# The second expert table of the sample, layer 0: row sums on VectorE in place of 32-column matmuls

## The chip, the cores and the metric

One Trainium2 chip; the kernel runs on one of its cores. The metric is the device time of one execution in microseconds. A core has a TensorE (PE; its weight loads are listed apart as PEld), a VectorE (DVE), a ScalarE (ACT), a GpSimd (POOL) and a SyncE (SP). SP and POOL here only issue transfers: SP those with fixed addresses, POOL the gathers. Each engine works through its own instruction list in order.

## The reference

Two layers, run over 512 prompt tokens and 128 sample tokens (8 streams of 16). Each layer has a mixer (layer 0: a gated convolution beside windowed attention; layer 1: a gated recurrence) and then a PEER channel mixer, which is what the change touches:

```python
def one_block(xb):                                   # 128 tokens
    q = (xb @ w_query).reshape(TB, 8, 2, 128)
    s = einsum('thpd,hpkd->thpk', q, keys)           # scores against 2 x 128 sub-keys, 8 heads
    sv, si = top_k(s, 16)
    cand = sv[:, :, 0, :, None] + sv[:, :, 1, None, :]
    cand_idx = si[:, :, 0, :, None] * 128 + si[:, :, 1, None, :]
    cv, ci = top_k(cand.reshape(TB, 8, 256), 16)
    idx = take_along_axis(cand_idx.reshape(TB, 8, 256), ci, axis=-1)
    gate = softmax(cv, axis=-1)
    act = gelu(einsum('thkd,td->thk', u_tab[idx], xb))   # first table: 16384 rows of 1024
    return einsum('thk,thkd->td', gate * act, v_tab[idx])    # second table
```

So every token chooses 8 x 16 = 128 experts; each gives a dot product with a row of the first table and adds a weighted row of the second. All is float32.

## The kernel before

The 640 tokens are five groups of 128: the sample ("s"), the prompt's first 128 tokens ("t") and the other 384 ("a", three groups). Groups s and t are computed **sparsely**: POOL gathers one row per token and expert slot. Group a is computed **densely**: all 16384 experts are multiplied with all 384 tokens, 128 experts at a time, and the weights are a matrix that is zero where an expert was not chosen.

The **sparse** part (`sparse_peer`, L823) first turns the ranking of sub-keys into row numbers and gates (`select`, L776, VectorE throughout). Then, for 128 slots, POOL gathers a tile `gu` of 128 rows (one per token, 1024 columns, 0.5 MB) of the first table into one of six buffers (tag "g") and VectorE takes the dot product with the token (L855). The second table follows in one of two ways, by the entry of `SUM` for the group and layer. With a tile name, `weighted` (L877): per slot a gather `gv` by the same row numbers, and one VectorE instruction that multiplies the 128 rows by their tokens' weights and adds to the sum `yv` (L891, the first one without an addition L889); at the end eight transposes and two additions into the activations (L872). With None, which only the sample in layer 0 has, `multiplied` (L903): row numbers and weights are transposed, a gather now fetches the 128 rows of one *token*, and TensorE sums over the partitions with a column of 32 weights of which one is not zero (L933; the column is a window of a zero ring `zr` into which VectorE copies the weights, L926). Four matmuls, for two tokens and two halves of 1024 columns, use four separate 32-column parts of the array and one PSUM bank.

Around that in layer 0 stands this program: `route_p` (L746) ranks the prompt's sub-keys, 16 projections on TensorE and 64 rankings on VectorE (`best`, L738). Then `found` (L970) builds the weight matrix of the three dense groups, 16 **one-hot steps** each, 48 in all. A step takes eight tokens: VectorE makes `ohb` (L988) and six of the `oha` (L1012), ScalarE makes two of them (L1009, L1010), TensorE multiplies them (L1014), ScalarE evacuates into `st` (L1017), and after four steps SP stores two tiles of 1 MB to DRAM (`gd`, L1020). `st` has two buffers. Beside all this run 72 **products ahead** (`ahead`, L956): scores of the last 72 of the 128 expert blocks, each with a load of 0.5 MB (`wraw`), a split into two parts on ScalarE and VectorE (L211, L212 `wlo`), 24 matmuls (L262 to L264), a Gelu (L967) and a store (`sd`, L968). Then the **dense loop** runs over the 128 blocks: its scores are multiplied with `gch`, the weights read back from `gd` (L1050), and then with the second table (L1062).

What stands where is decided twice. The program takes a fixed number of sparse slots per step of other work (`gather`, L1105; `GR` and `GS` are 8 for each projection and each of 12 steps after the routing, `PACE` 3 or 4 per block of the dense loop) and gives them a later priority. From this a scheduler with its own timing of the engines writes each engine's list, and the engines keep to it. The group t begins after the sample is done, with the dense loop; the sample's layer 1 begins at block 56 of it.

Of the kernel before, what the change touches and what calls it, by code (L numbers as in the profile page):

```python
# [8 lines left out]
F32 = mybir.dt.float32  # L9
F32R = mybir.dt.float32r  # L10
I32 = mybir.dt.int32
U32 = mybir.dt.uint32
U16 = mybir.dt.uint16
AF = mybir.ActivationFunctionType
# [4 lines left out]
NEG = -1e30  # L19
LOW = -3e38  # L20
NG = 6
NZ = 3
PACE = ((4,4,4,0)*10+(4,)*90,(3,))
THR = (1, 1, 1)
GM, GR, GS = ((4,),(1,)*40+(2,)*60), (8,8), (8,8)
# [16 lines left out]
LG = 4  # L42
DEEP = (54, 126)
LW = (1000, 1000)
RS = 0
SUM = dict(s=(None, "xn"), t=("vm", "vm"))
KQ = (-1, -1)
FE = ((12, 5, 72), (12, 5, 82))

# [12 lines left out]
def kernel(ctx: ExitStack, tc: tile.TileContext, t: dict):  # L62
    nc = tc.nc
    V, S, P, T, Y = nc.vector, nc.scalar, nc.gpsimd, nc.tensor, nc.sync

    con = ctx.enter_context(tc.tile_pool(name="con", bufs=1))
# [2 lines left out]
    dr = ctx.enter_context(tc.tile_pool(name="dr", bufs=1, space=bass.MemoryType.DRAM))  # L69

    BUFS = {"u4": 2, "uh": 2, "lo": 2, "v4": 4, "vh": 2, "w3": 2, "ge": 2, "g8": 2,
            "nat": 2, "g": NG, "sq": 2, "at": 2, "ai": 5, "vm": 1, "bt": 2, "bi": 2, "el": 2, "els": 2, "ln": 1,
            "gatea": 2, "mr": 1, "xa": 2, "xb": 4}

    def tl(tag, shape, dt=F32, name=None):
        return sb.tile(shape, dt, name=name or tag, tag=tag, bufs=BUFS.get(tag, 1))
# [4 lines left out]
    def bank(tag):  # L81
        return ps.tile([128, 512], F32, name="p" + tag, tag=tag, bufs=1)

    def gps(who):
        turn[who] = turn.get(who, -1) + 1
        return bank(banks[who][turn[who] % len(banks[who])])
# [18 lines left out]
    ident = con.tile([128, 128], F32, name="ident")  # L105
# [50 lines left out]
    V.tensor_tensor(lbt[:, 4], lbt[:, 4], lbt[:, 1], op=OP.subtract)  # L156
    V.tensor_scalar(lbt[:, 5], lbt[:, 4], -1.0, 1.0, op0=OP.mult, op1=OP.add)
    lb, oml = lbt[:, 4], lbt[:, 5]

    zring = []  # L160
    for i in range(NZ):
        z = con.tile([128, 2, 63], F32, name=f"zr{i}")
        V.memset(z, 0.0)
        zring.append(z)


    lay = tl("lay", [128, 1536])
# [652 lines left out]
        k2 = kf.rearrange("p s h k -> p s (h k)")  # L820
        return k2[:, 0], k2[:, 1], gate.rearrange("p h k -> p (h k)")

    def sparse_peer(G, l, xhl, sv, si, quad, acc=None):  # L823


        who = G.name
        xn = tl("xn", [128, 1024], name="xnn")
        for hf in range(2):
            p = gps(who)
            for u in range(4):  # L830
                for v in range(2):
                    T.matmul(p[:, 128 * u:128 * u + 128], xhl(v, 4 * hf + u), identr, start=(v == 0), stop=(v == 1))
            S.activation(xn[:, 512 * hf:512 * hf + 512], p, AF.Copy)
        k1, k2, gate = select(who, sv, si, quad)
        idf = tl("idf", [128, 128])
        V.scalar_tensor_tensor(idf, k1, 128.0, k2, op0=OP.mult, op1=OP.add)
        idt = None
        if acc is None:
            tp = gps(who)[:, :128]
            T.transpose(tp, idf, ident)  # L840
            idt = tl("bt", [128, 128], I32, name="idt")
            V.tensor_copy(idt, tp)
        yield 1
        idx = tl("bi", [128, 128], I32, name="idx")
        after(V.tensor_copy(idx, idf))  # L845
        w = tl("wact", [128, 128])
        rows = []
        for s in range(128 + LG):
            if s < 128:
                rows.append(tl("g", [128, 1024], name="gu"))  # L850
                P.indirect_dma_start(out=rows[s], out_offset=None, in_=t["u"][l],  # L851
                                     in_offset=bass.IndirectOffsetOnAxis(ap=idx[:, s:s + 1], axis=0))
            if s >= LG:
                g = rows[s - LG]
                d = V.tensor_tensor_reduce(out=g, in0=g, in1=xn, scale=1.0, scalar=0.0, op0=OP.mult, op1=OP.add,  # L855
                                           accum_out=w[:, s - LG:s - LG + 1])
                if paced[0] == 2:
                    after(d, 4 - s % 4)
                elif s % 4 == 0 and paced[0]:
                    after(d)  # L860
            yield 1
        S.activation(w, w, AF.Gelu)
        V.tensor_tensor(w, w, gate, op=OP.mult)
        if acc is not None:
            yield from weighted(G, l, idx, w, acc)
        else:
            yield from multiplied(G, l, idt, w)

    def put(G, l, hf, t0, n, q):

        xv = G.x[:, 4 * hf:4 * hf + 4, G.c0 + t0:G.c0 + t0 + n]
        V.tensor_tensor(xv, xv, q, op=OP.add)  # L872
        if l and t0 + n == 128:
            o0 = 512 if G is GS_ else G.c0
            Y.dma_start(t["o_y"][:, 4 * hf:4 * hf + 4, o0:o0 + 128], G.x[:, 4 * hf:4 * hf + 4, G.c0:G.c0 + 128])

    def weighted(G, l, idx, w, acc):  # L877

        y = tl(acc, [128, 1024], name="yv")
        rows = []  # L880
        for s in range(128 + LG):
            if s < 128:
                rows.append(tl("g", [128, 1024], name="gv"))
                P.indirect_dma_start(out=rows[s], out_offset=None, in_=t["v"][l],  # L884
                                     in_offset=bass.IndirectOffsetOnAxis(ap=idx[:, s:s + 1], axis=0))
            if s >= LG:
                e = s - LG
                if e == 0:
                    d = V.tensor_scalar(y, rows[e], w[:, e:e + 1], None, op0=OP.mult)  # L889
                else:  # L890
                    d = V.scalar_tensor_tensor(y, rows[e], w[:, e:e + 1], y, op0=OP.mult, op1=OP.add)  # L891
                if paced[0] == 2:
                    after(d, 4 - s % 4)
                elif s % 4 == 0 and paced[0]:
                    after(d)
            yield 1
        for hf in range(2):
            q = gps("v").rearrange("p (k q) -> p k q", k=4)
            for u in range(4):
                T.transpose(q[:, u], y[:, 512 * hf + 128 * u:512 * hf + 128 * u + 128], ident)  # L900
            put(G, l, hf, 0, 128, q)

    def multiplied(G, l, idt, w):  # L903

        tp = gps("v")[:, :128]
        T.transpose(tp, w, ident)
        wT = tl("wT", [128, 4, 32])
        S.activation(wT.rearrange("p c j -> p (c j)"), tp, AF.Copy)

        tok = [64 * rd + 32 * c + j for rd in range(2) for j in range(32) for c in range(2)]  # L910
        rows = []
        for s in range(128 + LG):
            if s < 128:
                rows.append(tl("g", [128, 1024], name="gv"))
                P.indirect_dma_start(out=rows[s], out_offset=None, in_=t["v"][l],  # L915
                                     in_offset=bass.IndirectOffsetOnAxis(ap=idt[:, tok[s]:tok[s] + 1], axis=0))
            yield 1
            if s < LG:
                continue
            i, c = tok[s - LG], (s - LG) % 2  # L920
            rd, j = i // 64, i % 32
            if c == 0:
                if j == 0:
                    y = gps("v")
                z = zring[j % NZ]
                d = V.tensor_copy(z[:, :, 31:32], wT[:, 2 * rd:2 * rd + 2, j:j + 1])  # L926
                if paced[0] == 2:
                    after(d, 4 - 2 * (j % 2))
                elif j % 2 == 0 and paced[0]:
                    after(d)  # L930
            for hf in range(2):
                q0 = 64 * hf + 32 * c
                T.matmul(y[q0:q0 + 32], z[:, c, 31 - j:63 - j], rows[s - LG][:, 512 * hf:512 * hf + 512], start=(j == 0),  # L933
                         stop=(j == 31), skip_group_check=True, tile_position=(0, q0))
            if j < 31 or c == 0:
                continue
            ys = tl("ln", [128, 512], name="ys")
            S.activation(ys, y, AF.Copy)
            q = gps("v").rearrange("p (k q) -> p k q", k=4)
            for u in range(4):  # L940
                T.transpose(q[:, u], ys[:, 128 * u:128 * u + 128], ident)
            for hf in range(2):
                put(G, l, hf, 64 * rd, 64, q[:, :, 64 * hf:64 * hf + 64])

    def dense_peer(l, xhl, sv, si):

# [147 lines left out]
    mark, paced = [None], [False]  # L1094

    def after(ins, back=0):

        m = marks[-back] if back and len(marks) >= back else mark[0]
        if m is not None:
            tc.add_manual_dep(ins.ins, m.ins.name, mybir.DependencyInfo(  # L1100
                mybir.DependencyClass.NoSync, mybir.DependencyReason.SCHED_ONLY), reason="order")
# [15 lines left out]
    def chain_s(l):  # L1117
# [10 lines left out]
        yield from route_s(l, xhl, sv, si, tags[0])  # L1128
        sp = sparse_peer(GS_, l, xhl, sv, si, tags[2], SUM["s"][l])
        next(sp)  # L1130
# [19 lines left out]
    for l in range(2):  # L1150
# [7 lines left out]
        while True:  # L1158
            w = next(order, "P")
# [15 lines left out]
        xhl = rmsnorm(GP, 1 + 2 * l)  # L1175
        banks.update({"p": ["y0", "y1", "y2", "y3"], "a": ["y0", "y1", "y2", "y3"], "h": ["s", "y5"]})
        sv, si = tl("v4", [128, 4, 16, 16], name="sv"), tl("w3", [128, 4, 16, 16], U16, name="si")
# [126 lines left out]
```

## Time and profile before

| | us |
|---|---|
| median of 3 runs | 4033.12 |
| lowest, highest | 4026.77, 4035.57 |
| profiled execution | 4031.51 |
| its span, first to last instruction | 4029.8 |

The profile is that of one execution. "Busy" is time in which an engine had an instruction under way; spans of neighbours overlap a little, and matmuls are pipelined with modelled ends, so a TensorE that is busy throughout need not be at its peak. [...] A window gives busy time per engine in a stretch; the timeline gives start, length, engine, line and operands of single instructions, merged where equal ones follow each other.

### The profile page before, as it was taken

How to read it: one execution, taken by the hardware profiler on the slowest of the kernel's cores; microseconds unless marked ns; L12 is line 12 of the kernel's file. 1: busy time of each engine (PE TensorE's matmuls, PEld its weight loads, DVE VectorE, ACT ScalarE, POOL GpSimd, SP SyncE). 2: the span in 40 equal slices, each digit the busy share in tenths (PEclk: the TensorE clock that was granted, in tenths of full speed). 3: DMA queues.
4: the chain of work that ended last, by engine and by line, in shares of the span. 5: the costliest groups of instructions: out<-in, count | busy, mean ns of one | idle time of the engine just before them, and what ended most of it. 6: DMA issues, size and time to landing. Idle time of an engine off the chain costs nothing.

```text
span 4029.8 us, 51936 instructions
## 1 busy us (share of the span) xinstructions
PE 3606.4 (89%) x17935; PEld 2962.0 (74%) x17935; DVE 3271.8 (81%) x6245; ACT 1723.3 (43%) x2915; POOL 1355.7 (34%) x1035
## 2 busy tenths in 40 slices
PE   6878778999999999778998878887999979999998
PEld 4756666779689997556766555566999969998776
DVE  5558999885468879887679887999998768888998
ACT  6644222467533334334344333232368953333333
POOL 0001665430245555541003552563000025444444
PEclk8989889999999999999999878798999979999999
DMA  4334998886789999998745775797445569999999
GB/s 143 116 111 161 337 338 315 313 333 234 275 297 338 338 333 356 371 356 286 236 164 202 259 238 177 253 323 264 147 156 211 209 233 343 341 335 354 385 385 332
DMA packets 454088, 1097.63 MB, mean 272 GB/s; under 512 B 36656, under 2 KB 233264, under 8 KB 447664
## 3 DMA queue, kind: packets, MB, share of 16 engines
q1 hardware_dynamic: 306368, 557.37, 40.0%
q0 software_dynamic: 147456, 536.94, 36.9%
q8 instruction: 141, 2.31, 0.2%
q14 instruction: 123, 1.01, 0.1%
HBM read 1005.92 MB, written 89.17 MB: 272 GB/s over the span
## 4 chain that ended last, share of the span: by engine, by line
PE 26%; DVE 13%; DMA 11%; issue 4%; ACT 3%; POOL 0%; SPq 0%; DVEq 0%; ACTq 0%; POOLq 0%
PE py L1062 10%; DMA sq<-sd 5%; DMA gu<-u,idx 3%; PE ps L255 3%; DVE wlo L212 2%; PE pb L255 2%; PE py L262 2%; DVE yv L891 2%; PE py L263 2%; PE py L264 2%; DVE gu L855 1%; PE ps L264 1%; PE ps L262 1%; PE ps L263 1%; PE ps L283 1%
## 5 line engine op out<-in xcount | busy, mean ns | idle before, releaser
L851 POOL DMA_INDIRECT gu<-u,idx x512 | 676.6, 1321 | 1791.4 <-DVE idx L845 871.7
L211 ACT ACTIVATE whi<-wraw 128x1024 fp32r<-128x1024 f32 x710 | 740.9, 1054 | 1034.6 <-PE py L263 311.2
L212 DVE TENSOR_TENSOR wlo<-wraw,whi 128x1024 fp32r<-128x1024 f32 x710 | 862.7, 1218 | 273.2 <-ACT whi L211 112.1
L1062 PE MATMUL py<-whi,wt 128*128 128x512 f32 x3072 | 794.9, 404 | 64.5 <-ACT wt L211 49.5
L1062 PEld LDWEIGHTS py<-whi,wt 128*128 128x128 f32 x3072 | 581.6, 192 | 216.1 <-ACT wt L211 61.5
L884 POOL DMA_INDIRECT gv<-v,idx x384 | 524.9, 1367 | 539.1 <-DVE yv L891 354.3
L855 DVE CUSTOM_DVE_ANT_0 gu<-gu,xnn 128x1024 f32<-128x1024 f32 x512 | 617.4, 1220 | 87.1 <-DMA gu<-u,idx 86.5
L262 PE MATMUL py<-xhl,whi 128*128 128x512 f32 (+1 forms) x1344 | 524.3, 391 | 72.7 <-ACT xhl L211 31.0
L264 PE MATMUL py<-xhl,wlo 128*128 128x512 f32 (+1 forms) x1344 | 518.2, 387 | 25.0 <-DVE wlo L212 24.7
L263 PE MATMUL py<-xhl,whi 128*128 128x512 f32 (+1 forms) x1344 | 515.8, 384 | 11.1 <-DVE xhl L212 11.0
L891 DVE SCALAR_TENSOR_TENSOR yv<-gv,wact,yv 128x1024 f32<-128x1024 f32 x381 | 487.6, 1280 | 2.6
L1062 PE MATMUL py<-wlo,wt 128*128 128x512 f32 x1536 | 400.0, 393 | 3.4 <-DVE wlo L212 3.4
L262 PE MATMUL ps<-xhl,whi 128*128 128x384 f32 (+1 forms) x1120 | 387.7, 346 | 7.3 <-ACT sm L481 3.7
L264 PE MATMUL ps<-xhl,wlo 128*128 128x384 f32 (+1 forms) x1120 | 387.2, 346 | 4.8 <-DVE wlo L212 4.7
L263 PE MATMUL ps<-xhl,whi 128*128 128x384 f32 (+1 forms) x1120 | 384.9, 344 | 0.0
L262 PEld LDWEIGHTS py<-xhl,whi 128*128 128x128 f32 x1344 | 266.4, 198 | 131.5 <-ACT xhl L211 35.4
L1062 PEld LDWEIGHTS py<-wlo,wt 128*128 128x128 f32 x1536 | 287.8, 188 | 70.5 <-DVE wlo L212 4.7
L264 PEld LDWEIGHTS py<-xhl,wlo 128*128 128x128 f32 x1344 | 265.6, 198 | 83.2 <-DVE wlo L212 35.7
L263 PEld LDWEIGHTS py<-xhl,whi 128*128 128x128 f32 x1344 | 265.7, 198 | 46.9 <-DVE xhl L212 15.4
L915 POOL DMA_INDIRECT gv<-v,idt x128 | 152.3, 1190 | 322.4 <-PE pb L933 295.2
L1017 ACT ACTIVATE st<-py 128x256 f32<-128x256 f32 x384 | 210.0, 665 | 84.4 <-PE py L1014 59.1
L262 PEld LDWEIGHTS ps<-xhl,whi 128*128 128x128 f32 x1120 | 213.6, 191 | 21.7 <-ACT ge L967 4.2
(435 smaller groups left out, 5014.3 us busy)
## 6 DMA issues: line engine op xcount, KB each, us to landing
wraw<-uT SPq DMA_DIRECT2D x256, 512.0 KB, 5.8
wraw<-v SPq DMA_DIRECT2D x256, 512.0 KB, 7.6
wraw<-w SPq DMA_DIRECT2D x98, 512.0 KB, 5.8
gd<-st SPq DMA_DIRECT2D x48, 1024.0 KB, 6.8
gch<-gd SPq DMA_DIRECT2D x64, 768.0 KB, 11.1
wraw<-wq SPq DMA_DIRECT2D x64, 512.0 KB, 6.3
sd<-ge SPq DMA_DIRECT2D x154, 192.0 KB, 3.5
ge<-sd SPq DMA_DIRECT2D x114, 192.0 KB, 8.1
```

What stands on the lines that cost most here:

```text
L211: S.activation(hi, src, AF.Copy)
L212: return V.tensor_tensor(lo, src, hi.bitcast(F32), op=OP.subtract)
L255: m = T.matmul(p, w[wv][:, k], xhl(xv, k), start=(k == 0 and xv == wv), stop=(k == 7 and wv == 1))
L262: T.matmul(p, w[0][:, k], xhl(0, k), start=(k == 0), stop=False)
L263: T.matmul(p, w[0][:, k], xhl(1, k), start=False, stop=False)
L264: T.matmul(p, w[1][:, k], xhl(0, k), start=False, stop=(k == 7))
L851: P.indirect_dma_start(out=rows[s], out_offset=None, in_=t["u"][l], in_offset=bass.IndirectOffsetOnAxis(ap=idx[:, s:s + 1], axis=0))
L855: d = V.tensor_tensor_reduce(out=g, in0=g, in1=xn, scale=1.0, scalar=0.0, op0=OP.mult, op1=OP.add, accum_out=w[:, s - LG:s - LG + 1])
L884: P.indirect_dma_start(out=rows[s], out_offset=None, in_=t["v"][l], in_offset=bass.IndirectOffsetOnAxis(ap=idx[:, s:s + 1], axis=0))
L891: d = V.scalar_tensor_tensor(y, rows[e], w[:, e:e + 1], y, op0=OP.mult, op1=OP.add)
L1017: S.activation(st[i][:, :, o0:o0 + 4].rearrange("p k t -> p t k"), p[:, :, 64 * i:64 * i + 64], AF.Copy)
L1062: mult[1] = T.matmul(yp[a][hf], wt[:, wv, 128 * a:128 * a + 128], vh[vv][:, 512 * hf:512 * hf + 512], start=(k == 0 and wv == 0 and vv == ...
```

## The change

`SUM` gets the tile "vm" for the sample in layer 0, so its second table goes through `weighted`, like t in both layers and the sample in layer 1. `multiplied`, the zero ring and the transposed row numbers are gone. The gathers are as many and as large; what a gather fetches is now one row for each token.

```diff
-SUM = dict(s=(None, "xn"), t=("vm", "vm"))
+SUM = dict(s=("vm", "xn"), t=("vm", "vm"))
...
-    zring = []
-    for i in range(NZ):
-        z = con.tile([128, 2, 63], F32, name=f"zr{i}")
-        V.memset(z, 0.0)
-        zring.append(z)
...
-        idt = None
-        if acc is None:
-            tp = gps(who)[:, :128]
-            T.transpose(tp, idf, ident)
-            idt = tl("bt", [128, 128], I32, name="idt")
-            V.tensor_copy(idt, tp)
...
-        if acc is not None:
-            yield from weighted(G, l, idx, w, acc)
-        else:
-            yield from multiplied(G, l, idt, w)
+        yield from weighted(G, l, idx, w, acc)
...
-    def multiplied(G, l, idt, w):
...
-                z = zring[j % NZ]
-                d = V.tensor_copy(z[:, :, 31:32], wT[:, 2 * rd:2 * rd + 2, j:j + 1])
...
-            for hf in range(2):
-                q0 = 64 * hf + 32 * c
-                T.matmul(y[q0:q0 + 32], z[:, c, 31 - j:63 - j], rows[s - LG][:, 512 * hf:512 * hf + 512], start=(j == 0),
-                         stop=(j == 31), skip_group_check=True, tile_position=(0, q0))
```

Since the scheduler writes the lists anew, they move too, from the ranking of the prompt to the start of the dense loop. Two places on VectorE show how. The line numbers of the changed kernel are smaller: L875 there is L891 here, L205 is L212, L930 is L988, L954 is L1012, and 732 to 737 are 739 to 744.

VectorE while the prompt is ranked, just after the last dot product of the sample; `sv` and `si` are values and places of the best sub-keys. Before:

```order
L742 MATCH_REPLACE mr<-sv,py_4243 128x128
L739 MAX sv<-py_4243 128x8
L926 COPY zr_115<-wT 128x2
L743 MAX sv<-mr 128x8
L926 COPY zr_117<-wT 128x2
L926 COPY zr_119<-wT 128x2
L740 MAX_INDEX si<-sv,py_4243 128x8
L744 MAX_INDEX si<-sv,mr 128x8
L212 TENSOR_TENSOR wlo<-wraw,whi 128x1024
```

Now:

```order
L875 SCALAR_TENSOR_TENSOR yv<-gv,wact,yv 128x1024
L733 MAX_INDEX si<-sv,py_4352 128x8
L737 MAX_INDEX si<-sv,mr 128x8
L205 TENSOR_TENSOR wlo<-wraw,whi 128x1024
L875 SCALAR_TENSOR_TENSOR yv<-gv,wact,yv 128x1024
L735 MATCH_REPLACE mr<-sv,py_4233 128x128
L732 MAX sv<-py_4233 128x8
L875 SCALAR_TENSOR_TENSOR yv<-gv,wact,yv 128x1024
L736 MAX sv<-mr 128x8
```

Between the short instructions of a ranking stand full-width sums where copies of two columns stood; 103 of the 128 sums stand ahead of the first one-hot step, and the last of them ahead of the 17th.

VectorE in the one-hot steps, around the 26th step before and from the 32nd now:

```order
L988 TENSOR_TENSOR ohb<-iota,tr 128x1024
L212 TENSOR_TENSOR wlo<-wraw,whi 128x1024
L1012 TENSOR_SCALAR oha<-iota,tr 128x128 x6
L988 TENSOR_TENSOR ohb<-iota,tr 128x1024
L1012 TENSOR_SCALAR oha<-iota,tr 128x128 x3
L212 TENSOR_TENSOR wlo<-wraw,whi 128x1024
L1012 TENSOR_SCALAR oha<-iota,tr 128x128 x3
```

Now:

```order
L930 TENSOR_TENSOR ohb<-iota,tr 128x1024
L954 TENSOR_SCALAR oha<-iota,tr 128x128 x6
L930 TENSOR_TENSOR ohb<-iota,tr 128x1024 x2
L954 TENSOR_SCALAR oha<-iota,tr 128x128 x12
L930 TENSOR_TENSOR ohb<-iota,tr 128x1024
```

The splits of the products ahead have left these steps: 133 splits of the whole program stood ahead of the 17th step, now 159 do. On POOL the list is the same but for the name of the row numbers.

## Rows read from the trace of the kernel before

**Rows 1.** The page, part 1: busy time, share of the span, instructions.

```profile
PE 3606.4 (89%) x17935; PEld 2962.0 (74%) x17935; DVE 3271.8 (81%) x6245; ACT 1723.3 (43%) x2915; POOL 1355.7 (34%) x1035
```

**Rows 2.** Windows: each stretch's busy time by engine, then granted clock and DMA.

```profile
core 0: us, PE busy (x) PEld busy (x) DVE busy (x) ACT busy (x) POOL busy (x), PEclk, DMA share, GB/s
375.00:634.00 259.00, 195.86 (x860) 162.84 (x860) 248.93 (x658) 57.47 (x73) 166.57 (x133) 0.87 0.94 338
634.00:753.00 119.00, 113.73 (x633) 79.42 (x631) 108.83 (x423) 32.91 (x48) 57.28 (x49) 0.98 0.89 319
634.00:879.00 245.00, 239.51 (x1424) 179.12 (x1423) 220.53 (x715) 114.88 (x219) 104.56 (x87) 0.99 0.87 315
879.00:1078.00 199.00, 199.00 (x1275) 178.83 (x1274) 120.66 (x256) 139.16 (x305) 29.14 (x23) 1.00 0.70 257
375.00:1114.00 739.00, 657.66 (x3663) 527.94 (x3662) 597.16 (x1644) 322.44 (x618) 313.02 (x256) 0.95 0.85 308
```

**Rows 3.** Windows of L933 (PE, PEld) and, below, of L926 (DVE) alone.

```profile
634.00:879.00 245.00, 63.83 (x344) 10.66 (x344) 0.99 0.87 315
375.00:1114.00 739.00, 103.34 (x508) 16.76 (x508) 0.95 0.85 308
...
634.00:879.00 245.00, 7.91 (x46) 0.99 0.87 315
375.00:1114.00 739.00, 11.13 (x64) 0.95 0.85 308
```

**Rows 4.** The page, part 5: busy us, mean ns, idle before and its releaser.

```profile
L884 POOL DMA_INDIRECT gv<-v,idx x384 | 524.9, 1367 | 539.1 <-DVE yv L891 354.3
L891 DVE SCALAR_TENSOR_TENSOR yv<-gv,wact,yv 128x1024 f32<-128x1024 f32 x381 | 487.6, 1280 | 2.6
L915 POOL DMA_INDIRECT gv<-v,idt x128 | 152.3, 1190 | 322.4 <-PE pb L933 295.2
```

**Rows 5.** L891 by itself: least, median and longest duration in ns.

```profile
L891 DVE SCALAR_TENSOR_TENSOR yv<-gv,wact,yv x381: 1165/1280/1328, 1501.9 to 4016.5; 128x1024 f32<-128x1024 f32 x191
```

**Rows 6.** Groups of VectorE instructions from 375 to 1114 us, columns as in rows 4.

```profile
L212 DVE TENSOR_TENSOR wlo<-wraw,whi 128x1024 fp32r<-128x1024 f32 x93 | 113.3, 1218 | 28.3 <-ACT whi L211 28.3
...
L811 DVE TENSOR_TENSOR oh<-oh,si 128x1024 f32<-128x1024 f32 x16 | 19.3, 1219 | 0.0
```

**Rows 7.** Timeline of VectorE and of SP's stores: start us, length us, instruction.

```profile
633.30 1.21 DVE L855 CUSTOM_DVE_ANT_0 gu<-gu,xnn 128x1024 f32<-128x1024 f32 x1
...
878.75 2.35 DVE L988 TENSOR_TENSOR ohb<-iota,tr 128x1024 f32<-128x1024 f32 x2
...
1078.06 1.22 DVE L988 TENSOR_TENSOR ohb<-iota,tr 128x1024 f32<-128x1024 f32 x1
...
1089.96 0.98 SPq L1020 DMA_DIRECT2D gd<-st  x2
...
1113.64 0.56 DVE L1050 TENSOR_TENSOR ge<-ge,gch 128x384 f32<-128x384 f32 x1 [14.11 <-DMA gch<-gd]
...
3271.26 2.10 SPq L1020 DMA_DIRECT2D gd<-st  x2
...
3283.07 0.56 DVE L1050 TENSOR_TENSOR ge<-ge,gch 128x384 f32<-128x384 f32 x1 [11.09 <-DMA gch<-gd]
```

**Rows 8.** Groups of ScalarE instructions from 879 to 1078 us, columns as in rows 4.

```profile
L1017 ACT ACTIVATE st<-py 128x256 f32<-128x256 f32 x116 | 64.6, 671 | 38.1 <-PE py L1014 34.5 <-DMA gd<-st 3.7
...
L1010 ACT ACTIVATE oha<-oha,tr 128x128 f32<-128x128 f32 x61 | 28.5, 493 | 0.6
L1009 ACT ACTIVATE oha<-iota,tr 128x128 f32<-128x128 f32 x62 | 23.2, 377 | 6.7 <-issue 3.7 <-PE py L1014 2.3 <-ACT ge L967 0.7
```

**Rows 9.** A window of layer 1's last one-hot steps, columns as in rows 2.

```profile
3251.00:3272.00 21.00, 14.51 (x64) 13.96 (x64) 14.18 (x12) 19.08 (x52) 0.00 (x0) 0.50 0.32 126
```

More of the change, by code (lines that the diff above doesn't have):

```diff
@@ L21 @@
 NG = 6
-NZ = 3
 PACE = ((4,4,4,0)*10+(4,)*90,(3,))
@@ L71 @@
     BUFS = {"u4": 2, "uh": 2, "lo": 2, "v4": 4, "vh": 2, "w3": 2, "ge": 2, "g8": 2,
-            "nat": 2, "g": NG, "sq": 2, "at": 2, "ai": 5, "vm": 1, "bt": 2, "bi": 2, "el": 2, "els": 2, "ln": 1,
+            "nat": 2, "g": NG, "sq": 2, "at": 2, "ai": 5, "vm": 1, "bi": 2, "el": 2, "els": 2, "ln": 1,
             "gatea": 2, "mr": 1, "xa": 2, "xb": 4}
@@ L821, in select, with sparse_peer @@
         return k2[:, 0], k2[:, 1], gate.rearrange("p h k -> p (h k)")
-    def sparse_peer(G, l, xhl, sv, si, quad, acc=None):
+    def sparse_peer(G, l, xhl, sv, si, quad, acc):
         who = G.name
@@ L901, in weighted @@
             put(G, l, hf, 0, 128, q)
-    def multiplied(G, l, idt, w):
[L905 to L924, printed above, removed]
-                z = zring[j % NZ]
-                d = V.tensor_copy(z[:, :, 31:32], wT[:, 2 * rd:2 * rd + 2, j:j + 1])
[L927 to L930, printed above, removed]
-            for hf in range(2):
-                q0 = 64 * hf + 32 * c
-                T.matmul(y[q0:q0 + 32], z[:, c, 31 - j:63 - j], rows[s - LG][:, 512 * hf:512 * hf + 512], start=(j == 0),
-                         stop=(j == 31), skip_group_check=True, tile_position=(0, q0))
[L935 to L943, printed above, removed]
     def dense_peer(l, xhl, sv, si):
```

## The prediction

> **What bounds the kernel now.** I read the busy shares first, then the stretches, then the timeline at their edges. Over the whole span TensorE's matmuls are busy 89% and VectorE 81% [rows 1], but the change touches one stage only, from about 375 us (the sample's row numbers are ready) to 1113.6 us (the first product of the dense loop). In that stage three regimes follow each other [rows 2]. Until 634 us the 128 dot products with rows of the first table run beside the prompt's ranking, and VectorE is busy 248.9 of 259 us, 96%. From 634 to 753 us VectorE and TensorE are both above 90%. From 879 to 1078 us TensorE is busy in every microsecond and VectorE only 120.7 of 199. So the bound moves from VectorE to TensorE inside the stage, and VectorE's whole idle time there is 739 - 597.2 = 142 us. After it TensorE carries the dense loop.
>
> **What goes.** The 256 matmuls with 32 columns (512 passes in the trace) keep TensorE busy for 103.3 us of the stage, and the copies of weights into the zero ring take VectorE 11.1 us [rows 3]. The index and the weights are no longer transposed and evacuated; these are four single instructions, set to nothing, as are the writes into xs, two of 512 columns in place of four of 256.
>
> **What comes.** 127 instructions that multiply a gathered row by a weight and add it, and one that only multiplies. Three groups of the kernel do this already: 1280 ns each [rows 4], 1165 at the least [rows 5]. That is 127 x 1.28 + 0.7 = 163 us of VectorE; 149 us by the least. [...]
>
> **The budget.** VectorE's work in the stage becomes 597.2 - 11.1 + 163 = 749 us (735 by the least duration). The stage lasts 739 us today. Even an unbroken VectorE would end about 10 us later (4 us earlier by the least). What decides is how much of its idle time can be used, and that is a matter of order.
>
> **The order.** In the changed program all 128 sums stand before the 17th of the 48 one-hot steps of layer 0. The products that are computed ahead moved forward with them: 159 weight splits stand before that step instead of 133, and TensorE, which no longer has the small matmuls, takes all but the last seven of the 72 products before it. So the TensorE-bound stretch after 879 us, where the idle VectorE time was, is emptied of the very work that filled it, and the sums went to where VectorE was full. I cost it in two pieces.
>
> Up to the 17th step. From the end of the dot products at 634 us to the step's start, today at 878.75 us [rows 7], VectorE works 220.5 us [rows 2]. Take off 7.9 of copies [rows 3], add 163 of sums, add 26 splits at 1.22 = 32 [rows 6], and take off about 20 for the last part of one selection (four each of three instructions at 1.22 us, such as L811 [rows 6], and small ones), which now stands behind the step. That is 388 us; instructions of different lines overlap by a few hundredths of a microsecond, so I take 385. At the 96% of the stretch before 634 us it lasts 401 us, at the 91% of 634 to 753 us 423, unbroken 385. Nothing else asks for more. TensorE had 239.5 us of work there, loses 63.8 [rows 2, 3] and gains some 23 products of at most 199/28 = 7.1 us, the time that a step with about one of them takes today: 339 us. The DMA engines moved 315 GB/s x 245 us = 77 MB there; 41 more gathers of 0.52 MB (87 of 128 stood in it [rows 2]) and 23 products' loads and stores of 0.72 MB make 115 MB, 287 GB/s over 401 us, below the 338 of the stretch before. On SP's queue their loads and stores now stand ahead of the score stores of later steps, which come later themselves. The step starts at 634 + 401 = 1035 us, against 879.
>
> From the 17th step to the end of the 48th. Today each step takes 199/31 = 6.4 us, TensorE's time for its share of products. Without them what is left per step is VectorE's 85/31 = 2.7 us (120.7 less 28 splits and copies [rows 2, 6]), and ScalarE's evacuations and one-hots, (64.6 + 28.5 + 23.2)/29 = 4.0 us [rows 8]. VectorE also has the 20 us of selection. Bounds for 32 steps: 107 us, VectorE alone with nothing lost; and 160 us, from layer 1, where the last four steps stand without products and take 20 us, at a granted clock of 0.50 and with ScalarE busy 19.1 of 21 [rows 9]. Those steps put more on ScalarE, so I take the nearer row, 4.0 each: 128 us. The last scores leave for DRAM at 1035 + 128 = 1163 us, against 1090 [rows 7].
>
> The end. Today 23.7 us pass from that issue to the first product of the dense loop, with the last gathers of the sample still landing; in layer 1, with no gathers, 11.8 us [rows 7]. The sums are long done by then, so I take 12: the dense loop starts at 1175 us. This is the one gain on the path.
>
> The sum: 1175 - 1113.6 = 61 us later. The order of the dense loop and of all behind it is the same but for neighbours that swap places, its TensorE is busy throughout, and the sample's result is not asked for before step 56, so I see nothing that gives the 61 us back. The profiled execution took 4031.5 us; 4031.5 + 61 = 4092.5. The median shown is 1.6 us above the profiled one, which is less than I can tell.
>
> **Rivals.** (a) Faster: TensorE is what counts. If the stage were bound by TensorE throughout and the sums fell into VectorE's idle 142 us, the whole 103.3 us would go: 4031.5 - 103 = 3928 us. It decides itself by VectorE's load: it needs the sums to stand among the one-hot steps after 879 us, or to cost under (739 - 586)/128 = 1.19 us without any idle time. For it: TensorE's 199 of 199 us. Against it: the 96% before 634 us, the 1280 ns of the row, and the order. [...] (b) Small: the one-hot tail runs at VectorE's bare pace and the front without a gap: 634 + 385 + 107 + 12 = 1138, 24 us later, 4056 us; with sums at the least duration 15 us lower, 4041. For it: VectorE's instructions abut in the saturated stretch. Against it: each one-hot step hands over from VectorE to TensorE to ScalarE to a DMA and back through two buffers. (c) Large: the front starves. Six row buffers now hang on a VectorE whose sums stand between rankings, and a gather's descriptors take POOL 1367 ns beside such sums, not 1190 [rows 4]; with VectorE at 91% and the tail at layer 1's pace the dense loop starts at 634 + 423 + 160 + 24 = 1241 us, 127 us later, 4159 us. Against it: at 385 us for 128 rows a gather is due every 3 us, twice POOL's time. (d) No change: the delay is swallowed later, by a wait that ends by itself; the trace has none on the dense loop's path.
>
> **How the numbers follow.** Forecast (30 to 100 us later) 0.75; (b) 0.10, half of it within what can be told from no change; (c) 0.08; (a) or another gain 0.05; (d) 0.02. About 0.2% of the time, 8 us, is what a measurement of this kernel can tell from no change. Faster 0.05, same 0.07, slower 0.88. For the range I leave the outer part of (c) and all of (a) and (d) out: from 4050, the middle of (b), to 4135, two thirds of the way from the forecast to (c).
>
> **What would show it.** In the changed profile: the sums at about 1.28 us, all between 634 us and about 1030; VectorE over 93% busy up to there; the 17th one-hot step near 1035 us and not 879; then steps of about 4 us with TensorE far from full and a granted clock under 0.9; 12 us from the last score issue to the dense loop, and the dense loop itself as long as before. I am wrong if the 17th step starts before 1000 us (sums cheaper than their row), if the tail takes under 105 or over 160 us, or if the dense loop of layer 0 gets shorter or longer by over 10 us.

## The result and the profile after

| | us |
|---|---|
| before, median of 4 runs on the chip of the comparison | 4034.35 (4026.77 to 4039.23) |
| after, median of 4 runs | 4086.04 (4083.5 to 4091.33) |
| ratio after to before | 1.0132, 95% interval 1.0112 to 1.0151 |
| profiled execution after, its span | 4084.94, 4083.2 |

The changed kernel is 1.3% slower. The forecast was 4092.5 us, 61 us later; 53 us were measured between the two profiled executions.

In the page's first part TensorE's matmuls lose 50.9 us against [rows 1] and VectorE gains 135.2:

```profile
PE 3555.5 (87%) x17421; PEld 2975.9 (73%) x17421; DVE 3407.0 (83%) x6303; ACT 1723.8 (42%) x2912; POOL 1379.5 (34%) x1035
```

The timeline after, at the same edges as [rows 7] (start, length, engine, line; L842 is the dot product, L930 a one-hot step, L962 the score store, L992 the first product of the dense loop):

```profile
635.52 1.20 DVE L842 CUSTOM_DVE_ANT_0 gu<-gu,xnn 128x1024 f32<-128x1024 f32 x1
...
1019.42 2.34 DVE L930 TENSOR_TENSOR ohb<-iota,tr 128x1024 f32<-128x1024 f32 x2
...
1145.83 1.22 DVE L930 TENSOR_TENSOR ohb<-iota,tr 128x1024 f32<-128x1024 f32 x1
...
1154.28 0.79 SPq L962 DMA_DIRECT2D gd<-st  x2
...
1167.24 0.56 DVE L992 TENSOR_TENSOR ge<-ge,gch 128x384 f32<-128x384 f32 x1 [10.45 <-DMA gch<-gd]
```

The last dot product starts 2.2 us later than before, the 17th step 140.7 us later, the 48th 67.8, the last stores 64.3 and the dense loop 53.6. The loss is made before the 17th step, and more than half of it is won back behind it. From there on little moves: the first product of layer 1's dense loop starts at 3333.8 us, 50.7 later than in [rows 7], and the end comes 53.4 us later.

Windows after, to be read against [rows 2] (columns as there; PEclk is the clock granted to TensorE, as a share of its full speed):

```profile
376.00:636.00 260.00, 192.01 (x860) 160.05 (x859) 248.81 (x659) 57.49 (x73) 168.40 (x133) 0.90 0.93 336
636.00:755.00 119.00, 74.30 (x371) 71.18 (x370) 118.84 (x276) 24.24 (x34) 77.99 (x63) 0.79 0.96 356
636.00:1019.00 383.00, 305.67 (x1702) 296.11 (x1701) 371.08 (x767) 150.49 (x268) 174.28 (x124) 0.90 0.84 305
1019.00:1146.00 127.00, 86.95 (x569) 77.63 (x567) 108.59 (x276) 105.00 (x257) 0.00 (x0) 0.93 0.37 148
...
376.00:1167.00 791.00, 590.35 (x3159) 539.13 (x3157) 733.69 (x1708) 322.44 (x616) 342.68 (x256) 0.90 0.79 287
```

Up to the last dot product little changed. Then VectorE (third number) is busy 371.1 of 383 us, 97%, where it was busy 220.5 of 245 (and TensorE, now at 305.7 of 383, 239.5 of 245); right behind the dot products it is 118.84 of 119. In the one-hot steps behind the 17th no engine is full. The sums themselves, as a group of instructions from 376 to 1167 us (busy us, mean ns, idle before and its releaser), answer to [rows 4]:

```profile
L875 DVE SCALAR_TENSOR_TENSOR yv<-gv,wact,yv 128x1024 f32<-128x1024 f32 x127 | 161.6, 1273 | 2.9 <-DMA gv<-v,idx 2.9
```

They are all done by 988 us, cost what their row of before said, and VectorE waited 2.9 us in all for a gathered row.

### The profile page after: what moved, and what is told of

The parts are those of the page before. It is cut to its first block, busy times and chain, and to the rows that moved or that the text cites. A ratio compares the mean times of both kernels' runs of the same rounds, so it can differ in the third digit from the quotient of the medians.

```text
span 4083.2 us, 51017 instructions
## 1 busy us (share of the span) xinstructions
PE 3555.5 (87%) x17421; PEld 2975.9 (73%) x17421; DVE 3407.0 (83%) x6303; ACT 1723.8 (42%) x2912; POOL 1379.5 (34%) x1035
## 3 DMA queue, kind: packets, MB, share of 16 engines
q14 instruction: 125, 1.02, 0.1%
## 4 chain that ended last, share of the span: by engine, by line
PE 46%; DVE 24%; DMA 13%; issue 9%; ACT 7%; POOL 1%; SPq 0%; DVEq 0%; ACTq 0%; POOLq 0%
PE py L1004 16%; DMA ge<-sd 5%; DVE wlo L205 5%; DVE yv L875 4%; PE ps L257 3%; PE ps L255 3%; PE ps L256 3%; DVE gu L842 3%; PE py L255 3%; PE py L257 3%; PE py L256 3%; DMA gu<-u,idx 3%; PE ps L248 3%; PE pb L248 2%; ACT st L959 2%
## 5 line engine op out<-in xcount | busy, mean ns | idle before, releaser
L205 DVE TENSOR_TENSOR wlo<-wraw,whi 128x1024 fp32r<-128x1024 f32 x710 | 860.9, 1216 | 264.1 <-ACT whi L204 100.6
L868 POOL DMA_INDIRECT gv<-v,idx x512 | 706.5, 1380 | 693.2 <-DVE yv L875 388.5
L1004 PEld LDWEIGHTS py<-whi,wt 128*128 128x128 f32 x3072 | 582.5, 193 | 235.2 <-ACT wt L204 79.6
L842 DVE CUSTOM_DVE_ANT_0 gu<-gu,xnn 128x1024 f32<-128x1024 f32 x512 | 616.3, 1218 | 75.4 <-DMA gu<-u,idx 74.4
L875 DVE SCALAR_TENSOR_TENSOR yv<-gv,wact,yv 128x1024 f32<-128x1024 f32 x508 | 648.6, 1277 | 5.5 <-DMA gv<-v,idx 2.9
L255 PE MATMUL py<-xhl,whi 128*128 128x512 f32 (+1 forms) x1344 | 530.0, 395 | 83.3 <-ACT xhl L204 31.2
L256 PE MATMUL py<-xhl,whi 128*128 128x512 f32 (+1 forms) x1344 | 521.6, 388 | 11.3 <-DVE xhl L205 11.2
L255 PEld LDWEIGHTS py<-xhl,whi 128*128 128x128 f32 x1344 | 271.4, 202 | 136.3 <-ACT xhl L204 35.5
L256 PEld LDWEIGHTS py<-xhl,whi 128*128 128x128 f32 x1344 | 270.8, 201 | 50.0 <-DVE xhl L205 15.7
L257 PEld LDWEIGHTS ps<-xhl,wlo 128*128 128x128 f32 x1120 | 214.2, 191 | 15.2 <-DVE wlo L205 11.1
```

Source lines behind the costliest of these rows:

```text
L205: return V.tensor_tensor(lo, src, hi.bitcast(F32), op=OP.subtract)
L255: T.matmul(p, w[0][:, k], xhl(0, k), start=(k == 0), stop=False)
L256: T.matmul(p, w[0][:, k], xhl(1, k), start=False, stop=False)
L257: T.matmul(p, w[1][:, k], xhl(0, k), start=False, stop=(k == 7))
L1004: mult[1] = T.matmul(yp[a][hf], wt[:, wv, 128 * a:128 * a + 128], vh[vv][:, 512 * hf:512 * hf + 512], start=(k == 0 and wv == 0 and vv == ...
```

## The experiments

Each kernel below is the changed one with one edit, one of them with two. All were timed with the kernel before on the same chip; the ratios are to it, where the changed kernel's is 1.0132. Theory W is that of the prediction: VectorE's work sets the stage.

**No sums.** The instruction is left out, the gathers are not.

```diff
+                elif G is GS_ and l == 0:
+                    d = None
                 else:
                     d = V.scalar_tensor_tensor(y, rows[e], w[:, e:e + 1], y, op0=OP.mult, op1=OP.add)
...
```

> Left out: 127 of the 128 sums with the second table for the sample in layer 0 (only the first, multiplying one stays; all gathers stay). Theory W (VectorE's work sets the stage from the last dot product, 637 us, to the dense loop, 1167 us): the sums are 127 x 1.273 = 162 us there; VectorE is busy 371 of the 383 us before the 17th one-hot step and hardly less behind it, so most of the 162 goes until TensorE's work (some 570 us from 376 us on, now 590 of 791) and VectorE's own (734 - 162 = 572) are level: 110 to 150 us less, 3935 to 3975 us. Theory O (not the work but the order costs: the one-hot steps stand without products ahead): the order here keeps products ahead among the last steps, so the 53 us come back, 4033 us, and no more. Theory G (the gathers on GpSimd pace the sums): the gathers are as many, so 4080 to 4090 us.

Measured: 4018.44 us, ratio 0.9972 (0.9961 to 0.9984). The dense loop starts at 1086.8 us, 80.4 earlier than with the sums and 26.8 earlier than with the 32-column matmuls. Windows from the last dot product to the 17th step, and from there to the last:

```profile
638.00:847.00 209.00, 157.49 (x865) 146.42 (x864) 204.56 (x657) 103.96 (x207) 143.78 (x119) 0.89 1.02 405
847.00:1062.00 215.00, 196.09 (x1234) 190.73 (x1235) 123.42 (x250) 140.73 (x304) 8.78 (x5) 0.98 0.59 216
```

The gathers do not pace the changed kernel: with no sum to wait for they were issued beside transfers of 405 GB/s in all, against 305, so theory G falls. The 162 us of sums cost 80 us of the stage, not the 110 to 150 that I expected of W, and the reason is in the second line: without them the products ahead stay among the last steps, and TensorE is busy 196 of 215 us there. This kernel also gives the worth of TensorE's relief alone. Without the 103.3 us of small matmuls *and* without sums the stage is only 27 us shorter than before. Up to the 17th step it is 36 us shorter, and there VectorE is full again (204.6 of 209); the DMA engines are full too (a share of 1.02), but VectorE idles for only 4.4 us there, and more than that they cannot have held it up. From the 17th step to the 48th it takes 215 us in place of 199. Since the lists are written anew for each kernel, that is the worth as scheduled here. Of the 80 us, 22 are lost again between the last block of the dense loop and layer 1 in the profiled execution, which was the longest of seven (4026.21 us); what ends last there I did not follow. By its time alone this run does not tell W from O: 4018 lies nearer O's 4033. The next ones do.

**Sums without the addition.**

```diff
-                if e == 0:
+                if e == 0 or G is GS_ and l == 0:
                     d = V.tensor_scalar(y, rows[e], w[:, e:e + 1], None, op0=OP.mult)
```

> Changed: each sum of the sample in layer 0 only multiplies the row by its weight and does not add (one tensor-scalar instruction of 128x1024 with one source in place of the multiply-add with two); gathers, count and places in the program as before, though the order moves. From the trace a one-source instruction of this size takes about 0.75 us, so each is 0.52 us cheaper. Theory W: 127 x 0.52 = 66 us of VectorE's work go, the time falls by 50 to 66 us: 4020 to 4036 us, back to where the 32-column matmuls were. Theory G (gathers pace the sums): no change, 4080 to 4090 us. The rival of the prediction that TensorE's relief counts below 1.19 us per sum would now be on the faster side of the kernel with matmuls: 3930 to 4000 us.

Measured: 4037.11 us, ratio 1.0013 (0.9999 to 1.0026): back at the kernel before. The group of these instructions, and the windows to the 17th step and over the stage:

```profile
L873 DVE TENSOR_SCALAR yv<-gv,wact 128x1024 f32<-128x1024 f32 x128 | 95.2, 743 | 1.2 <-DMA gv<-v,idx 1.1
```

```profile
636.00:903.00 267.00, 215.68 (x1213) 207.08 (x1212) 259.18 (x708) 117.49 (x223) 135.39 (x96) 0.90 0.87 317
...
375.00:1113.00 738.00, 582.53 (x3159) 536.01 (x3157) 667.68 (x1707) 320.42 (x616) 338.60 (x256) 0.90 0.85 308
```

VectorE has 667.7 us of work in the stage in place of 733.7, 66.0 less, and the dense loop starts at 1113.4 us, 53.8 earlier. The lists moved too, but with the same gathers and nearly the same TensorE work (582.5 and 590.4 us) the time follows VectorE's; 4037 is 1 us above W's range. It also prices the change: an instruction of 743 ns breaks even with the matmuls, one of 1273 does not. My bound for rival (a), faster below 1.19 us, was far too kind.

**Sums held back to the one-hot steps.** An order-only dependence; nothing else is touched.

```diff
+                if G is GS_ and l == 0 and fm[0] is not None:
+                    follow(d, fm[0])          # fm[0]: the latest ohb
...
```

> Nothing left out: each of the sample's sums of layer 0 is held, by order alone, behind the one-hot step beside which the program gives it; 36 stand before the first of the 48 steps (103 in the changed kernel), 103 before the last, 111 before the dense loop. The gathers keep their count. Theory W: VectorE's work up to the dense loop is the same but for 17 sums (22 us); its idle time in the stretch from 376 to 1167 us is 57 us, so the gain is 22 to 50 us: 4036 to 4064 us. Theory O (the place of the sums is what costs; among the last one-hot steps they would fall into idle time of VectorE and let TensorE's relief through): 103 us below the changed kernel or more, under 3985 us.

Measured: 4068.99 us, ratio 1.0096 (1.0078 to 1.0113). The dense loop starts at 1135.4 us, 31.8 earlier, and takes 979.4 us in place of 962.5: the 17 sums that leaked into it (22 us of VectorE) cost 17 there. Windows before and behind the 17th step:

```profile
636.00:924.00 288.00, 241.54 (x1400) 235.24 (x1399) 279.72 (x697) 129.94 (x240) 78.61 (x61) 0.91 0.71 251
924.00:1105.00 181.00, 141.26 (x864) 131.51 (x863) 171.08 (x319) 124.43 (x285) 58.17 (x44) 0.93 0.81 290
```

Now VectorE is full on both sides of the 17th step (97% and 95%). The time lies 5 us above W's range and far above O's. The order, with the 22 us of sums that left the stage by it, was worth some 15 us of the 53 (by the ratios; 17 by the medians), so O falls as the main cause. It also says how little an order can win: with all sums in the stage VectorE has 734 us of work there, and the whole stage of the kernel before lasts 739.

**Sums moved into the dense loop.** The program gives the sample two slots per step in place of eight.

```diff
-GM, GR, GS = ((4,),(1,)*40+(2,)*60), (8,8), (8,8)
+GM, GR, GS = ((4,),(1,)*40+(2,)*60), (8,8), (2,8)
```

> Nothing left out: the program gives the sample 2 slots instead of 8 for each of the 12 steps behind the routing, so that 60 of its 128 sums stand before the dense loop and 68 in its first 30 blocks, where VectorE is busy 348 of 437 us. Theory W: 68 x 1.273 = 87 us of VectorE's work leave the stage, the dense loop starts 55 to 85 us sooner (1082 to 1112 us), and its first blocks have 89 us of idle VectorE time for 87 us of sums: 4005 to 4035 us if they fit, up to 4070 us if about half of it is lost again there. Rival L (work moved into the dense loop lengthens it by as much, since VectorE and the DMA engines are near their limits there): 4080 to 4095 us.

Measured: 4104.67 us, ratio 1.018 (1.0158 to 1.0202), slower than the changed kernel and above the ranges of both theories. The first half of W held: the dense loop starts at 1108.2 us, 59.0 earlier, and its first 64 blocks are no longer, although the sums stand in them. Windows of the stage, the first 64 blocks and the others, of this kernel and then of the changed one:

```profile
634.00:1108.00 474.00, 383.11 (x2290) 370.55 (x2288) 405.01 (x977) 263.24 (x543) 77.21 (x61) 0.90 0.63 226
1108.00:1641.00 533.00, 514.98 (x2514) 455.17 (x2514) 451.94 (x606) 198.76 (x273) 262.83 (x193) 0.98 0.95 339
1641.00:2121.00 480.00, 396.59 (x1702) 300.77 (x1703) 403.87 (x626) 183.67 (x247) 175.46 (x126) 0.92 0.91 322
```

```profile
636.00:1167.00 531.00, 398.35 (x2301) 379.08 (x2299) 484.88 (x1050) 264.96 (x543) 174.28 (x124) 0.90 0.72 263
1167.00:1701.00 534.00, 515.60 (x2506) 454.83 (x2506) 438.47 (x601) 199.83 (x274) 265.92 (x190) 0.99 0.94 336
1701.00:2130.00 429.00, 375.93 (x1656) 285.32 (x1655) 329.14 (x513) 175.55 (x239) 94.20 (x66) 0.96 0.85 297
```

The other 64 blocks take 51 us more, and the way from the last block to layer 1's dense loop 26 us more (1230 against 1204). In the last blocks POOL issues 126 transfers, not 66: in the first blocks the sample's rows took the slots of group t, whose own rows moved back to the last blocks. Either the sums or the places could be the cause, which the next kernel tells apart.

**The same without the sums.** The edits of the first and the fourth kernel together.

> Left out: as in nosum, 127 of the 128 sums of the sample in layer 0; and the program gives the sample 2 slots per step behind the routing, as in gs2, so that 68 of its gathers fall into the dense loop and the other sparse group t begins as late as in gs2. It tells what made gs2's dense loop 51 us longer than the changed kernel's (1013 against 962 us from its first product to that of the last block) and the way from there to layer 1's first dense product 26 us longer. Theory V (the 68 sums themselves, VectorE's work): both lengths fall back, the loop to 955 to 970 us, the rest by 15 us or more; whole time 4005 to 4030 us. Theory P (not the sums but the places: group t's rows of the second table, its gathers and sums pushed from blocks 48 to 88 into blocks 64 to 112, and what of layer 1 waits for t): the loop stays 995 to 1013 us and the rest is no shorter; whole time 4060 to 4090 us.

Measured: 4082.54 us, ratio 1.0133 (1.0108 to 1.0159). Without a single moved sum the loop is as long as with them (1018 us against 1013), and the way to layer 1 takes 1224 us against 1230. The sample's gathers were to fall into the loop but did not: with no sum to wait for, the last one started at 856 us. Group t still began late, and all 128 of its sums of layer 0 stand in the last 64 blocks, as in the kernel above; in the changed kernel 74 do. Window of the last 64 blocks:

```profile
1619.00:2100.00 481.00, 399.87 (x1723) 307.22 (x1721) 404.15 (x626) 185.19 (x248) 176.53 (x128) 0.93 0.91 321
```

It is the line of the kernel above almost to the digit. So the longer loop comes from the places: group t's rows, gathers and sums, come beside the last blocks. Which of these sets the pace there was not tried. For the 26 us on the way to layer 1 the places are not shown to be the cause: without sums that way takes as long with the sample's old places (1226 us, the first kernel). That stays open.

**One-hots shared differently.** Two kernels test what bounds the 32 steps behind the 17th: `SHARE` 2 lets ScalarE make four of eight one-hots, `SHARE` 5 none.

```diff
-SHARE = (3, 3)
+SHARE = (2, 3)      # the other kernel: (5, 3)
```

> Nothing left out: of the eight one-hots that a step multiplies, ScalarE makes four in layer 0, not two (two instructions of 0.38 and 0.49 us each), VectorE four, not six (0.28 us each where they follow each other). Theory S (without products ahead the last 32 one-hot steps are bound by ScalarE, as the 4.0 us per step of the prediction were worked out): ScalarE's 105 us of the tail's 135 become about 160, the tail 160 to 180 us, the front some 9 us shorter: 4100 to 4125 us. Theory H (the tail is bound by VectorE, or by the hand-over between engines): the tail does not get longer, VectorE has 18 us less there and 9 in front: 4060 to 4080 us.

> Nothing left out: VectorE makes all eight one-hots of a step in layer 0, ScalarE none. VectorE's work grows by 2 x 0.28 us per step, 9 us up to the 17th step and 18 us in the 32 behind it; ScalarE loses 55 us in the tail. Theory S (tail bound by ScalarE): the tail falls to VectorE's 127 us or a little more, the front grows by 9: 4080 to 4092 us. Theory H (VectorE or the hand-over): the tail grows with VectorE to 145 to 155 us, with the front 4100 to 4115 us.

Measured: four on ScalarE 4118.18 us, ratio 1.0215 (1.0194 to 1.0235), and none 4091.1, ratio 1.0141 (1.0119 to 1.0163). From the 17th step to the second of the two last stores 166.5 and 132.8 us, against 135.3 in the changed kernel. Windows of these steps, with four and then with none:

```profile
1003.00:1157.00 154.00, 115.03 (x649) 104.66 (x647) 98.33 (x218) 145.67 (x385) 0.00 (x0) 0.86 0.39 151
```

```profile
1030.00:1156.00 126.00, 79.26 (x548) 73.20 (x547) 121.64 (x341) 66.02 (x132) 0.00 (x0) 0.91 0.37 144
```

With more on ScalarE it is full (fourth number, 145.7 of 154), and the steps take 31 us longer for 41 us more of its work, since it had been idle for 22 of 127. With nothing on it VectorE is full (121.6 of 126) and the steps take about as long as before. Both times lie in the ranges of theory S; but the changed kernel's mixture, VectorE 108.6 and ScalarE 105.0 of 127 us, is close to even between the two, so taking work from ScalarE alone gains nothing. With four on ScalarE the 17th step came 16 us earlier, with none 10 later: VectorE's work once more. The first of the two is 32 us slower by the medians; its profiled execution, the shortest of four, is 24 us longer, of which 14 are there at the dense loop's start and 21 at layer 1's. Where the others arise I did not follow.

Over all these kernels the stretch from the last dot product to the 17th step follows VectorE's work, whatever the work is. The kernel before, with 220.5 of 245 us [rows 2], stands apart, since TensorE was full there as well:

| | stretch, us | VectorE busy in it, us |
|---|---|---|
| no sums | 209 | 204.6 |
| no sums, two slots per step | 209 | 204.6 |
| sums without addition | 267 | 259.2 |
| held back | 288 | 279.7 |
| moved to the dense loop | 304 | 299.5 |
| four one-hots on ScalarE | 368 | 357.8 |
| changed kernel | 383 | 371.1 |
| no one-hots on ScalarE | 393 | 378.9 |

The windows of the four that no line above shows, in the order of the table:

```profile
632.00:841.00 209.00, 158.01 (x868) 147.04 (x868) 204.56 (x659) 103.57 (x206) 140.81 (x118) 0.89 1.02 403
634.00:938.00 304.00, 250.07 (x1439) 242.63 (x1437) 299.49 (x739) 136.55 (x251) 77.21 (x61) 0.90 0.69 246
635.00:1003.00 368.00, 288.97 (x1615) 277.59 (x1614) 357.82 (x728) 164.33 (x323) 171.28 (x123) 0.90 0.84 304
637.00:1030.00 393.00, 308.42 (x1717) 296.56 (x1717) 378.94 (x792) 132.35 (x207) 180.24 (x123) 0.90 0.83 298
```

## Why the prediction was right, step by step

- **What bounds.** Right where the sums went: between the dot products and the 17th step VectorE is busy 97% in place of 90%. TensorE was fuller still there, 98% [rows 2], and is now at 80%, so this front passed from both engines to VectorE alone. TensorE's full stretch behind the 17th step was emptied by the order.
- **Price of a sum.** 1280 ns taken from [rows 4], 1273 measured. The splits of the same size (L205) took 1214 ns here, 59 less, so the multiply-add's own row was the one to use.
- **Up to the 17th step.** 385 us of work at 96%, 401 us, were predicted; 371.1 at 97%, 383, were measured. This is the term that was mis-sized, by 18 us: some 14 because there was less work, some 4 because VectorE was fuller. Much of the first is overlap. In the run without sums VectorE is busy 586 us in its stage and 734 with the sums, 148 more for 127 instructions whose own busy time is 161.6. The trace shows the same directly: a sum starts 0.08 us before its predecessor on VectorE ends, and the two one-hots at 1019.42 us above take 2.34 us where one takes 1.22. For the sums alone that is some 11 us; I had allowed 3 us in all.
- **Behind the 17th step.** 32 steps of 4.0 us, 128, against 134.9 to the first of the two last stores. The row that it was made from, ScalarE's in [rows 8], was the right place to look, as the kernel with four one-hots on ScalarE shows; but VectorE is nearly as full, and the two hand over through TensorE, as the longest waits of this stretch say (engine, line, what it waited for, us, times, longest):

```profile
PEld py L956 <- ACT oha L952: 16.1, 24, 1.7
PEld py L956 <- ACT st L959: 14.2, 5, 3.2
PE py L956 <- ACT st L959: 13.2, 5, 3.0
PEld py L956 <- DVE oha L954: 12.0, 14, 4.6
DVE oha L954 <- PE py L956: 11.9, 14, 1.7
```

- **The end.** 12 us from the first of the two last stores to the dense loop, 13.0 measured. **Nothing given back:** from its first product to that of the 128th block the loop takes 962.5 us, against 965.1. A reason that I gave was half right: TensorE was busy 518.6 of 535 us in the first 64 blocks of the loop before, but 375.2 of 431 in the others. Windows of the kernel before, the later blocks first:

```profile
1648.00:2079.00 431.00, 375.24 (x1650) 283.36 (x1650) 330.24 (x513) 175.32 (x239) 87.25 (x66) 0.96 0.86 296
1114.00:1649.00 535.00, 518.61 (x2514) 455.16 (x2514) 439.07 (x604) 200.63 (x275) 273.02 (x191) 0.98 0.94 335
```

- **The sum.** The errors of -18 (front), +7 (steps), +1 (end) and +3 (the dot products end at 636.7 us, not 634) make 54 of 61 us at the dense loop's start, and 53 at the end. That the total is nearer than its largest term is luck: the errors partly cancel. The upper bound of the steps had been taken from layer 1 at a granted clock of 0.50 [rows 9], and I expected less than 0.9; it was 0.93. That sign of the list failed, without weight, since TensorE does not set the pace there.
- **Rivals.** (a) would have needed TensorE to count; the run without sums shows that its relief is worth 27 us of 103 even if the sums were free, as scheduled there. (b), 24 us, needed the steps at VectorE's bare pace; they took 135 us, not 107. (c) fell with the 2.9 us of waiting for rows and the 97% of VectorE. (d) did not occur.

## What to carry to other kernels

Before work is moved from one engine to another, split the stage into its regimes and ask which engine is full where the moved work will *stand*; a share over the whole span, here 89% against 81%, names the wrong engine. An engine's work in a stage beside the stage's length is the quickest test: 734 us of VectorE in a stage of 739 leaves next to nothing to win. And work that is pushed out of a full stage displaces what stood in the next one, so look for who is late there before counting the gain.

## What the runs showed of the hardware that I had not expected

Without the small matmuls TensorE's other work took longer. In the stage TensorE was busy 657.7 us before, 103.3 of them with the small matmuls [rows 2, 3]. The records of matmuls overlap a little: taken by themselves, the other matmuls of the trace cover 563.5 us, and in the changed kernel, where there are as many (3155 and 3159 in the two records), 590.4. So 27 us more went into the same work, and with 9 us of overlap gone too, TensorE was relieved of 67 us instead of 103. The one-hot products, before (375 to 1114 us) and after (376 to 1167 us), are among those that took longer, 277 and 295 ns each:

```profile
L1014 PE MATMUL py<-oha,ohb 128*128 128x128 f32 x768 | 105.3, 277 | 0.0
...
L956 PE MATMUL py<-oha,ohb 128*128 128x128 f32 x768 | 111.0, 295 | 39.7 <-ACT st L959 16.2 <-ACT oha L952 11.3 <-DVE oha L954 11.0
```

The granted clock of the stage, a mean over stretches at 0.50 and at 1.00 (after, for example, 0.50 from 645 to 680 us and 1.00 from 875 to 1005), fell from 0.95 to 0.90, and in the 119 us behind the dot products from 0.98 to 0.79, where TensorE's busy time fell from 113.7 to 74.3. That the clock is the cause of the 27 us was not tried by itself. Up to the 17th step they cost nothing that shows, since VectorE set the pace there.

The gathers' time on POOL differs from kernel to kernel: 1190 ns each before [rows 4], where a gather fetches the rows of one token, 1241 without sums, 1374 beside one-source multiplications, and 1406 beside the multiply-adds of the changed kernel. What sets it was not tried, and spans on POOL are rough. In the changed kernel the sums waited 2.9 us in all for their rows.
